# A latent convolution in 32x32 tiles of the TensorE array, and a layer norm with channels on the partitions

## The chip, the cores and the metric

The kernel runs on one core of one Trainium2 chip. The core has five engines that run their own instruction queues and meet at semaphores: TensorE (PE in the profile; PEld is its weight load), VectorE (DVE), ScalarE (ACT), GpSimd (POOL) and SyncE (SP), which here issues every DMA. Each engine takes its instructions in the order in which they stand in its queue. The metric is the time of one execution on the device in microseconds. Before the change it is 1876.82 us, the median of three runs (1874.78 to 1887.96).

## What is computed

One layer of a hybrid backbone over 2304 tokens (256 of a prompt, 2048 of a 32x64 grid of latents): an input projection, an SSD (Mamba-2) branch in both directions, a conformer branch, and an output projection over both branches. The change concerns the conformer branch alone:

```
def depthwise_conv(x, w, b):            # 31 taps along the rows of the grid
    k, ch = w.shape
    out = lax.conv_general_dilated(
        x, w.reshape(k, 1, 1, ch).astype(x.dtype), window_strides=(1, 1),
        padding=((k // 2, k // 2), (0, 0)),
        dimension_numbers=('NHWC', 'HWIO', 'NHWC'), feature_group_count=ch)
    return out + b.astype(x.dtype)
...
def conformer_branch(ga, gb, conv_w, conv_b, ln_g, ln_b):
    h = ga * jax.nn.sigmoid(gb)
    h = depthwise_conv(h, conv_w, conv_b)
    h = layer_norm(h, ln_g, ln_b)
    return jax.nn.silu(h)
...
    y_conf = y_conf.reshape(bsz, seqlen, D_CONF) * jax.nn.silu(gsil)
    out = jnp.concatenate([y_ssd.astype(x.dtype), y_conf.astype(x.dtype)], axis=-1) @ w_out
    return x + gate * rms_norm(out, g_post), h_fin
```

For the latents the grid has 32 rows and 64 columns, so the convolution of one channel is a 32x32 banded matrix applied to 64 columns. There are 1024 channels. The layer norm runs over the 1024 channels of a token.

## The kernel before

Tokens are handled in 18 tiles of 128 (two of the prompt, sixteen of the latents), channels in 8 groups of 128. The input projection runs in two halves of the tokens. In each half, units of matmuls of 128x512 (`xbc_unit`, `gab_unit`, `silu_unit`, with the matmuls on L378 to L380, three for each piece since every weight and activation is split in a high and a low part) form the backbone of TensorE's work, and smaller work is put between them: the forward scan (`pass_a`), the prompt's convolution on VectorE (`ctx_conv`) and the latent convolution on TensorE (`lat_conv`). `gab_unit` writes the gated channels to the DRAM buffers `GL[j]`.

`lat_conv(j)` runs for each group of 128 channels, in the second half of the tokens. It loads the banded matrices (`kd`) and the input (`x`) so that four channels share the 128 partitions, four times 32 rows of the grid. ScalarE spreads each block of 32x32 into a block diagonal matrix in one of two zeroed buffers `kbuf` (`expand`, L622, 16 copies for a group). A matmul on L634 then has `x` as its weights (128 rows, 64 columns) and `kbuf` as its moving operand (128 columns), and gives the result with the 64 grid columns on the partitions. VectorE adds the bias (L639), and two DMAs write the result to `CVL`, token by token.

The second stage, from about 1420 us to the end, is the output projection, one tile of 128 tokens after the other. For each tile there are 96 matmuls of 128x512 on L1078 (`out_part`): 48 on the SSD half `yh`, `yl`, 48 on the conformer half `ph`, `pl`. Between them the next tiles are prepared: `ssd_pre`, `ssd_norm`, `ssd_scale` for the SSD half; `conf_pre` loads a tile of the convolution's result with tokens on the partitions and normalizes it by statistics along the free axis (L1042 to L1047; the power of -0.5 of 128 single numbers is on POOL, L135), and `conf_act` turns it to channels on the partitions by eight transposes on TensorE (L1058), applies scale, bias and SiLU on ScalarE (L1061) and multiplies by the gate (L1063). `conf_hl` splits the result in `ph` and `pl`. The tiles `cn` (normalized), `v`, `ph`, `pl` have one buffer each.

The source sets what is computed and which buffers are used, and a list scheduler, which plays the program through with its own cost estimates when the program is built, sets the order of the instructions in each engine's queue. So the order of a queue is not the order of the source, and it is shown below, from the built programs.

Of the kernel before, what the change touches and what calls it, by code (L numbers as in the profile page):

```python
# [67 lines left out]
def backbone_kernel(ctx, tc, xa, xt_in, cols, rows, wconv, conf_b, gp_row, bg_row, state0, w_mod, w_dt, w_in, w_out,  # L68
# [458 lines left out]

    def gab_unit(half, j, hb):
        wb = next_w()
        wa = next_w()  # L530
        for b in ORDER[half]:
# [48 lines left out]
    def ctx_conv(j, tile):  # L580
# [22 lines left out]
    def lat_conv(j, lp, kbuf):  # L603
        cbb = lp.tile([P, HD], F32, tag="cbb", name=f"cbb{j}", bufs=2)
        for h in range(2):
            c0 = j * P + h * 64
# [8 lines left out]
        for c4 in range(4):
            DMA.dma_start(x[c4 * 32:(c4 + 1) * 32], src[c4])

        def expand(u):
            kt = kbuf[u % 2]
            for c4 in range(4):  # L620
                rs = slice(c4 * 32, (c4 + 1) * 32)
                S.copy(kt[rs, :, rs].rearrange("p (h q) r -> p h q r", h=2),  # L622
                       kd[rs].rearrange("p r (h u q) -> p u h q r", h=2, u=4)[:, u])
# [606 lines left out]
```

## Time and profile before

| what | value |
|---|---|
| median of three runs | 1876.82 us |
| the profiled execution, its own time | 1882.2 us |
| its span in the profile | 1880.5 us |
| TensorE busy | 1825.6 us, 97% of the span |
| VectorE, ScalarE, GpSimd busy | 63%, 45%, 14% |
| granted TensorE clock, mean | 0.986 |

In the profile a line such as L1078 is a line of the kernel before. Busy time of TensorE is time in which some matmul is under way; matmuls overlap, so the start of one to the start of the next, not the duration, says what one costs. A matmul of two float32 operands is two instructions in the trace (hence x16 for eight), one of float32r operands is one.

### The profile page before, as it was taken

How to read it: one execution, taken by the hardware profiler on the slowest of the kernel's cores; microseconds unless marked ns; L12 is line 12 of the kernel's file. 1: busy time of each engine (PE TensorE's matmuls, PEld its weight loads, DVE VectorE, ACT ScalarE, POOL GpSimd, SP SyncE). 2: the span in 40 equal slices, each digit the busy share in tenths (PEclk: the TensorE clock that was granted, in tenths of full speed). 3: DMA queues.
4: the chain of work that ended last, by engine and by line, in shares of the span. 5: the costliest groups of instructions: out<-in, count | busy, mean ns of one | idle time of the engine just before them, and what ended most of it. 6: DMA issues, size and time to landing. Idle time of an engine off the chain costs nothing.

```text
span 1880.5 us, 26833 instructions
## 1 busy us (share of the span) xinstructions
PE 1825.6 (97%) x9739; PEld 1504.6 (80%) x9739; DVE 1188.2 (63%) x1699; ACT 839.5 (45%) x1786; POOL 269.0 (14%) x351
## 2 busy tenths in 40 slices
PE   7899999999999999999999899999999999999998
PEld 4788887787887888888877677777887888888887
DVE  2477887776545553577585768655427676766662
ACT  3646424443455441644355666675414232232321
POOL 0002001111111100100001011110013333333220
PEclk9899999999999999999999999999999999999999
DMA  8556575564677754545587897978887655555532
GB/s 302 212 200 198 211 239 179 176 222 155 211 269 225 225 200 169 165 154 188 179 195 215 210 242 194 278 185 234 239 268 239 191 174 173 165 172 173 175 102 78
DMA packets 290400, 375.29 MB, mean 200 GB/s; under 512 B 85206, under 2 KB 187478, under 8 KB 290268
## 3 DMA queue, kind: packets, MB, share of 16 engines
q1 hardware_dynamic: 290268, 373.58, 64.2%
q8 instruction: 77, 1.26, 0.3%
q14 instruction: 55, 0.45, 0.1%
HBM read 243.92 MB, written 129.59 MB: 199 GB/s over the span
## 4 chain that ended last, share of the span: by engine, by line
PE 62%; DMA 5%; ACT 3%; issue 3%; DVE 2%; SPq 2%; POOL 0%; POOLq 0%; DVEq 0%; ACTq 0%
PE op L1078 20%; PE sp L378 6%; PE sp L379 6%; PE sp L380 6%; DMA lb<-lt 3%; PE xp L379 2%; PE xp L378 2%; PE xp L380 2%; PE py L720 2%; PE ga L378 2%; PE ga L380 1%; PE po L727 1%; PE ga L379 1%; PE qo L985 1%; PE gb L378 1%
## 5 line engine op out<-in xcount | busy, mean ns | idle before, releaser
L684 ACT ACTIVATE lb<-lb,WB 128x128 f32<-128x128 f32 x576 | 184.1, 391 | 150.9 <-POOL lb L676 149.0
L378 PE MATMUL sp<-hh,wh 128*128 128x512 f32 (+1 forms) x640 | 239.7, 375 | 2.6 <-DVE sth L550 2.6
L379 PE MATMUL sp<-hl,wh 128*128 128x512 f32 (+1 forms) x640 | 237.0, 370 | 0.0
L380 PE MATMUL sp<-hh,wl 128*128 128x512 f32 (+1 forms) x640 | 236.7, 370 | 0.2 <-DMA wl<-wld 0.2
L676 POOL TENSOR_SCALAR_AFFINE_SELECT lb<-lb 128x512 f32<-128x512 f32 x144 | 108.7, 760 | 749.7 <-ACT el L673 416.1
L378 PE MATMUL xp<-hh,wh 128*128 128x512 f32 (+1 forms) x480 | 179.1, 375 | 6.1 <-ACT wh L353 4.0
L379 PE MATMUL xp<-hl,wh 128*128 128x512 f32 (+1 forms) x480 | 179.1, 373 | 0.2 <-DVE hl L299 0.2
L380 PE MATMUL xp<-hh,wl 128*128 128x512 f32 (+1 forms) x480 | 179.2, 374 | 0.0
L475 DVE SCALAR_TENSOR_TENSOR cva<-raw,cwh,cva 128x1280 f32<-128x1280 f32 (+1 forms) x96 | 142.7, 1495 | 15.5 <-ACT cva L469 13.6
L378 PEld LDWEIGHTS sp<-hh,wh 128*128 128x128 f32 x640 | 121.0, 189 | 24.3 <-DVE sth L550 3.1
L380 PEld LDWEIGHTS sp<-hh,wl 128*128 128x128 f32 x640 | 121.0, 189 | 21.6 <-DMA wl<-wld 0.7
L379 PEld LDWEIGHTS sp<-hl,wh 128*128 128x128 f32 x640 | 121.2, 189 | 20.1 <-issue 0.5
L378 PE MATMUL gb<-hh,wh 128*128 128x512 f32 (+1 forms) x320 | 121.9, 381 | 3.4 <-DVE gth L539 3.4
L378 PE MATMUL ga<-hh,wh 128*128 128x512 f32 (+1 forms) x320 | 120.4, 376 | 2.6 <-ACT gth L536 2.6
L379 PE MATMUL gb<-hl,wh 128*128 128x512 f32 (+1 forms) x320 | 119.3, 373 | 0.0
L380 PE MATMUL gb<-hh,wl 128*128 128x512 f32 (+1 forms) x320 | 119.1, 372 | 0.0
L380 PE MATMUL ga<-hh,wl 128*128 128x512 f32 (+1 forms) x320 | 118.1, 369 | 0.0
L379 PE MATMUL ga<-hl,wh 128*128 128x512 f32 (+1 forms) x320 | 117.9, 369 | 0.0
L590 DVE SCALAR_TENSOR_TENSOR cg<-cg,cv 128x256 f32<-128x256 f32 x240 | 113.3, 497 | 2.5
L550 DVE SCALAR_TENSOR_TENSOR sth<-sth,sp 128x512 f32<-128x512 f32 (+1 forms) x80 | 50.4, 630 | 98.4 <-ACT sth L549 98.4
L378 PEld LDWEIGHTS xp<-hh,wh 128*128 128x128 f32 x480 | 92.0, 192 | 23.0 <-ACT wh L353 4.8
L688 DVE TENSOR_TENSOR lb<-lb,lb 128x512 f32<-128x512 f32 x72 | 51.6, 717 | 85.6 <-ACT lb L684 55.8
(219 smaller groups left out, 3860.8 us busy)
## 6 DMA issues: line engine op xcount, KB each, us to landing
lb<-lt SPq DMA_DIRECT2D x144, 256.0 KB, 4.2
wr<-in_w_in SPq DMA_DIRECT2D x88, 256.0 KB, 4.9
whd<-wh SPq DMA_DIRECT2D x44, 512.0 KB, 3.4
wld<-wl SPq DMA_DIRECT2D x44, 512.0 KB, 4.7
wh<-whd SPq DMA_DIRECT2D x44, 512.0 KB, 5.2
wl<-wld SPq DMA_DIRECT2D x44, 512.0 KB, 5.6
xT<-xb SPq DMA_DIRECT2D x18, 512.0 KB, 5.4
yp<-yg SPq DMA_DIRECT2D x36, 256.0 KB, 4.5
```

The source lines that it names most:

```text
L378: T.matmul(ps[:, :BN], wh[:, k, :], hh[:, k, :], start=(k == 0), stop=False)
L379: T.matmul(ps[:, :BN], wh[:, k, :], hl[:, k, :], start=False, stop=False)
L380: T.matmul(ps[:, :BN], wl[:, k, :], hh[:, k, :], start=False, stop=(k == KT - 1))
L475: V.scalar_tensor_tensor(a[:, :n], raw[:, t:t + n], cwh[:, ct * 5 + t:ct * 5 + t + 1], a[:, :n], MUL, ADD)
L550: V.scalar_tensor_tensor(th, th, 1.0, ps[:, :BN], ADD, MUL)
L590: V.scalar_tensor_tensor(acc, g[:, t:t + 256], cv[:, w0 + t:w0 + t + 1], acc, MUL, ADD)
L676: G.affine_select(E[g, hq, d], E[g, hq, d], pattern=[[0, 4], [sg, P]], compare_op=ALU.is_ge, fill=NEG, base=0, channel_multiplier=-sg)
L684: S.activation(lb[:, h, :], lb[:, h, :], AF.Exp, bias=WB[:, i, c + h:c + h + 1])
L688: V.tensor_tensor(a, a, E[g, hq, 1], ADD)
L720: T.matmul(py[g][j * HD:(j + 1) * HD, q * P:(q + 1) * P], xt[g][:, h * HD:(h + 1) * HD], E[g, hq, 0][:, t, :], start=True, stop=True)
L727: T.matmul(po[g][:, q * P:(q + 1) * P], Sf[g][:, q * P:(q + 1) * P], bc[:, 2 + g, :], start=True, stop=True)
L1078: T.matmul(pso[n], lhs[:, k % 8, :], w[:, n * 512:(n + 1) * 512], start=(k == 0 and m == 0), stop=(k == 15 and m == 2))
```

## The change

The convolution's weights are no longer block diagonal. Each matmul now takes one channel: a 32x32 banded matrix `kt` as weights in one 32x32 tile of the array, and the channel's 32 rows by 64 columns as the moving operand. Four channels stand on four groups of rows (`a`), and four groups of columns (`u`) give 16 places, of which a run of 64 matmuls uses two row groups and four column groups. There are 128 such matmuls for a group of 128 channels where there were 32. One copy on ScalarE reverses the band; `expand` and `kbuf` are gone; loads are issued a group ahead where `GL[j]` is complete (`lat_load`, `gl_done`), in 16 pieces instead of 4, and results are written in 8 pieces instead of 2. Results stand in one buffer `CV` with channels as rows, and the prompt's convolution writes there too, without its two transposes for a group.

In the output stage a tile is loaded with channels on the partitions (`conf_load`). The sum over 1024 channels is taken by three additions on VectorE and a matmul with ones (`quarter_sum`), once for the mean and once for the squares, which gives the sum on all partitions. The power of -0.5 on POOL is taken of 128x128 numbers. The eight transposes go. The steps are `conf_load`, `conf_mean`, `conf_var`, `conf_act`.

```diff
-    kbuf = [lp.tile([P, 8, P], F32, name=f"kbuf{u}") for u in range(2)]
-    for u in range(2):
-        G.memset(kbuf[u], 0.0)
...
@@ ctx_conv
-        ps = bank("ss", f"cps{j}")
-        for t in range(2):
-            T.transpose(ps[:, t * P:(t + 1) * P], acc[:, t * P:(t + 1) * P], ident)
         o = g[:, 768:1024]
-        S.mul(o, ps[:, :256], 0.5)
+        S.mul(o, acc, 0.5)
+        DMA.dma_start(CV[j * P:(j + 1) * P, 0:256], o)
...
@@ lat_conv (the old body is printed above)
+    def lat_load(j, lp):
+        kd = lp.tile([P, 32, 32], F32, tag="kd", name=f"kd{j}", bufs=2)
+        x = lp.tile([P, 32, 64], F32, tag="cx", name=f"cx{j}", bufs=2)
+        lat_in[j] = kd, x
+        for a in range(4):
+            rs = slice(a * 32, (a + 1) * 32)
+            src = bass.AP(tensor=wconv.tensor, offset=(j * 4 + a) * 64 * 32, ap=[[32, 32], [1, 1024]])
+            DMA.dma_start(kd[rs].rearrange("p r g -> p (r g)"), src)
+            for u in range(4):
+                c0 = u * 32 + a * 8
+                DMA.dma_start(x[rs, u * 8:(u + 1) * 8, :],
+                              GL[j][c0:c0 + 8, 256:].rearrange("c (r w) -> r c w", w=64))
+
+    def lat_conv(j, lp, cbb, more):
+        if j not in lat_in:
+            lat_load(j, lp)
+        kd, x = lat_in.pop(j)
+        yield
+        kt = lp.tile([P, 32, 32], F32, tag="kt", name=f"kt{j}", bufs=1)
+        S.copy(kt[:, :, ::-1].rearrange("p g r -> p r g"), kd)
+        if more(j + 1):
+            lat_load(j + 1, lp)
+        yield
+        vt = lp.tile([P, 32, 64], F32, tag="cvv", name=f"cvv{j}", bufs=1)
         for h in range(2):
+            ps = {a: bank("ss", f"cp{j}_{a}") for a in (2 * h, 2 * h + 1)}
+            for q in range(8):
+                for u in range(4):
+                    for a in ps:
+                        rs = slice(a * 32, (a + 1) * 32)
+                        T.matmul(ps[a][u * 32:(u + 1) * 32, q * 64:(q + 1) * 64], kt[rs, u * 8 + q, :], x[rs, u * 8 + q, :],
+                                 start=True, stop=True)
             yield
+            for a in ps:
+                V.scalar_tensor_tensor(vt[:, a * 8:(a + 1) * 8, :], ps[a].rearrange("p (c w) -> p c w", w=64), 0.5,
+                                       cbb[:, j, a * 8:(a + 1) * 8].unsqueeze(2).to_broadcast([P, 8, 64]), MUL, ADD)
+            for u in range(4):
+                c0 = j * P + u * 32 + h * 16
+                DMA.dma_start(CV[c0:c0 + 16, 256:].rearrange("c (r w) -> r c w", w=64),
+                              vt[u * 32:(u + 1) * 32, h * 16:(h + 1) * 16, :])
+            yield
...
+    def quarter_sum(t, v, name):
+        V.tensor_tensor(t, v[:, 0:4, :], v[:, 4:8, :], ADD)
+        V.tensor_tensor(t[:, 0:2, :], t[:, 0:2, :], t[:, 2:4, :], ADD)
+        V.tensor_tensor(t[:, 0, :], t[:, 0, :], t[:, 1, :], ADD)
+        ps = bank("ss", name)
+        T.matmul(ps[:, 0:P], ones, t[:, 0, :], start=True, stop=True)
+        return ps[:, 0:P]
...
+    def conf_mean(i, n):
+        v = p2.tile([P, 8, P], F32, tag="v", name=f"v{i}", bufs=1)
+        mean = quarter_sum(v[:, 0:4, :], n, f"cm{i}")
+        V.scalar_tensor_tensor(n, rows8(mean), -1.0 / D, n, MUL, ADD)
+        return n, v
+
+    def conf_var(i, nv):
+        n, v = nv
+        S.activation(v, n, AF.Square)
+        var = quarter_sum(v[:, 0:4, :], v, f"cq{i}")
+        r = p2.tile([P, P], F32, tag="cr", name=f"cr{i}", bufs=1)
+        V.tensor_scalar(r, var, 1.0 / D, EPS, MUL, ADD)
+        G.tensor_tensor(r, r, nhalf.to_broadcast([P, P]), ALU.pow)
+        V.tensor_tensor(n, n, rows8(r), MUL)
+        return n, v
...
@@ the loop over tiles
-            n = conf_pre(nxt)
-        out_part(pso[i], yh, 3, 6)
+            n = conf_load(nxt)
+        out_part(pso[i], yh, 3, 5)
         if not last:
             yhn = ssd_scale(nxt, yr)
-        out_part(pso[i], yh, 6, 8)
+        out_part(pso[i], yh, 5, 7)
+        if not last:
+            n = conf_mean(nxt, n)
+        out_part(pso[i], yh, 7, 8)
         out_part(pso[i], pt, 8, 10)
...
+            n = conf_var(nxt, n)
+            out_part(pso[i], pt, 10, 12)
             v = conf_act(nxt, n)
-            out_part(pso[i], pt, 10, 16)
+            out_part(pso[i], pt, 12, 16)
```

Three places of the built programs show how the queues change. The first is VectorE in the output stage, one tile of the steady part, before the change (lines of the kernel before; `bs`, `mv` and `cn` are the layer norm of one tile, `elb`, `y`, `z`, `zr` the SSD half of a tile two ahead, `o` the output being finished, `v` the conformer half):

```order
L1063 SCALAR_TENSOR_TENSOR v_13650<-v_13650,gsl_13648 128x1024
L1042 BN_STATS bs_13784<-cn_13782 128x6 x2
L1044 BN_AGGR mv_13787<-bs_13784 128x2
L1045 TENSOR_SCALAR mv_13787<-mv_13787 128x1
L1047 TENSOR_SCALAR cn_13782<-cn_13782,mv_13787,cr_13790 128x1024
L1070 TENSOR_TENSOR pl_13721<-v_13650,ph_13720 128x1024
L1006 TENSOR_SCALAR yms_13734<-pm_13732 128x1
L1088 TENSOR_TENSOR oms_13709<-oms_13709 128x1
L1089 TENSOR_SCALAR oms_13709<-oms_13709 128x1
```

The same queue with the change (lines of the changed kernel: L1068 gives the variance `cr` from the sum `cq`, L1070 multiplies the tile by its power, which POOL has taken in between, L1111 begins the finish of the output):

```order
L1068 TENSOR_SCALAR cr_15724<-cq_15722 128x128
L1010 TENSOR_SCALAR yms_15803<-pm_15801 128x1
L1105 TENSOR_TENSOR oms_15778<-oms_15778 128x1
L1106 TENSOR_SCALAR oms_15778<-oms_15778 128x1
L990 TENSOR_TENSOR elb_15821<-elb_15821,qo_15830 128x512
L990 TENSOR_TENSOR elb_15821<-elb_15821,qo_15836 128x512
L991 TENSOR_TENSOR y_15824<-y_15824,elb_15821 128x1024
L992 TENSOR_TENSOR y_15824<-y_15824,z_15826 128x1024
L995 TENSOR_REDUCE zr_15845<-z_15826 128x128
L1070 TENSOR_TENSOR cn_15661<-cn_15661,cr_15724 128x1024
L1111 SCALAR_TENSOR_TENSOR o_15777<-op_0_15603,or_15783,gg_13855 128x512
L1111 SCALAR_TENSOR_TENSOR o_15777<-op_1_15604,or_15783,gg_13855 128x512
```

Before, the layer norm of a tile stood in one piece and ended with `cn`, a tile ahead of its use; now its second half is spread over the tile's row, with the SSD half's work between `cr` and the multiplication.

The second place is TensorE in the same part, one tile with the change (`cm` and `cq` are the two sums over channels, `ph_15789` is the conformer half that comes out of the layer norm whose sums these are, `op` the output's banks):

```order
L1095 MATMUL op_1_15604<-woh_13814,ph_15599 128x512
L1047 MATMUL cm_15697<-v_15693,ones 128x128
L1095 MATMUL op_0_15603<-wol_13813,ph_15599 128x512
...
L1095 MATMUL op_1_15604<-wol_13849,ph_15599 128x512
L1047 MATMUL cq_15722<-v_15693,ones 128x128
L1095 MATMUL op_0_15603<-woh_13850,pl_15600 128x512
...
L1016 MATMUL pm_15801<-ident,yr_15805 128x128
...
L1095 MATMUL op_0_15793<-woh_13509,ph_15789 128x512
```

Between `cm` and `cq` stand 38 matmuls on L1095 (the former L1078), between `cq` and the first one on `ph_15789` 35 with the matmuls of `qo` and `pm`, and between that one and the next tile's `cm` 24. Before the change the same stretch held one interruption, and it came half a tile or more before its result was used:

```order
L1078 MATMUL op_0_13917<-woh_13066,pl_13914 128x512
L1078 MATMUL op_1_13918<-woh_13066,pl_13914 128x512
L1058 MATMUL ct_14037<-ident,cn_13975 128x128 x4
L1058 MATMUL ct_14046<-ident,cn_13975 128x128 x4
L1078 MATMUL op_0_13917<-woh_13072,ph_13913 128x512
L1078 MATMUL op_1_13918<-woh_13072,ph_13913 128x512
```

The eight transposes `ct` are gone, and two single matmuls have come, each of which waits for VectorE and is waited for by it.

The third place is the queue of DMAs (SP) during the latent convolution, with the change (`lb` are rows of decays that the forward scan loads and waits for, `cx` and `kd` the convolution's inputs, `cv` its results):

```order
L599 DMA cv<-cg_11250 128x256
L666 DMA lb_10049<-lt_116 128x512
L617 DMA cx_9768<-gl_71 32x8x64 x16
L645 DMA cv<-cvv_9834 32x16x64 x4
L666 DMA lb_10114<-lt_116 128x512
L666 DMA lb_10437<-lt_116 128x512
L599 DMA cv<-cg_12388 128x256
```

Here 20 DMAs of the convolution stand between two loads of the scan. In the queue before, the same loads and stores of a group (two halves) read like this:

```order
L616 DMA cx_9617<-gl_70 32x32x64 x2
L644 DMA cvl<-cvv_9297 64x32x64 x2
L616 DMA cx_9617<-gl_70 32x32x64 x2
L664 DMA lb_9716<-lt_117 128x512
L607 DMA cbb_10325<-in_conf_b 64x64 x2
L664 DMA lb_9799<-lt_117 128x512
```

The loads of the scan have moved behind longer groups of smaller DMAs.

More of the change, by code (lines that the diff above doesn't have):

```diff
@@ L526, in xbc_phase @@
             pass
+    gl_done = set()
     def gab_unit(half, j, hb):
@@ L530, in gab_unit @@
         wa = next_w()
+        gl_done.discard(j)
         for b in ORDER[half]:
@@ L540, in gab_unit @@
             DMA.dma_start(GL[j][:, o:o + BN], th)
+        if half:
+            gl_done.add(j)
     def silu_unit(half, c0, dst, j, hb, order=None):
@@ L928, in backbone_kernel @@
     lp = ph_l.enter_context(tc.tile_pool(name="lp", bufs=1, side="right"))
-    kbuf = [lp.tile([P, 8, P], F32, name=f"kbuf{u}") for u in range(2)]
-    for u in range(2):
-        G.memset(kbuf[u], 0.0)
+    cbb = lp.tile([P, 8, 32], F32, name="cbb")
+    for u in range(4):
+        DMA.dma_start(cbb[u * 32:(u + 1) * 32],
+                      conf_b.rearrange("(j u n) -> u j n", u=4, n=32)[u].partition_broadcast(32))
     blocks = post(1, 5)
     cg = lambda name: lp.tile([P, D], F32, tag="cg", name=name, bufs=2)
-    extra = chain(f for j in range(4) for f in (lat_conv(2 * j, lp, kbuf), ctx_conv(j + 4, cg), lat_conv(2 * j + 1, lp, kbuf)))
+    lat = lambda j: lat_conv(j, lp, cbb, gl_done.__contains__)
+    extra = chain(f for j in range(4) for f in (lat(2 * j), ctx_conv(j + 4, cg), lat(2 * j + 1)))
     sc_ = scan(range(9, NT))
@@ L1035, in load_gg @@
         gg[a] = t
-    def conf_pre(i):
-        n = p2.tile([P, D], F32, tag="cn", name=f"cn{i}", bufs=1)
-        DMA.dma_start(n, CVC[i * P:(i + 1) * P, :] if i < 2 else CVL[(i - 2) * P:(i - 1) * P, :])
-        bs = p2.tile([P, 12], F32, tag="bs", name=f"bs{i}", bufs=2)
-        for h in range(2):
-            V.bn_stats(bs[:, 6 * h:6 * h + 6], n[:, h * 512:(h + 1) * 512])
-        mv = p2.tile([P, 2], F32, tag="mv", name=f"mv{i}", bufs=2)
-        V.bn_aggr(mv, bs)
-        V.tensor_scalar(mv[:, 1:2], mv[:, 1:2], EPS, None, ADD)
-        r = rstd_of(p2, mv[:, 1:2], f"cr{i}")
-        V.tensor_scalar(n, n, mv[:, 0:1], r, SUB, MUL)
-        return n
@@ L1051, in conf_act @@
+    def conf_act(i, nv):
+        n, v = nv
         gs = p2.tile([P, 8, P], F32, tag="gs", name=f"gsl{i}", bufs=1)
         DMA.dma_start(gs, chan_slice(GS, i))
-        v = p2.tile([P, 8, P], F32, tag="v", name=f"v{i}", bufs=1)
-        for g in range(2):
-            ps = bank("ss", f"ct{i}{g}")
-            for c in range(4):
-                k = 4 * g + c
-                T.transpose(ps[:, c * P:(c + 1) * P], n[:, k * P:(k + 1) * P], ident)
-            for c in range(4):
-                k = 4 * g + c
-                S.activation(v[:, k, :], ps[:, c * P:(c + 1) * P], AF.Silu, bias=cv[:, C_LNB + k:C_LNB + k + 1],
-                             scale=cv[:, C_LNG + k:C_LNG + k + 1])
+        for k in range(8):
+            S.activation(v[:, k, :], n[:, k, :], AF.Silu, bias=cv[:, C_LNB + k:C_LNB + k + 1],
+                         scale=cv[:, C_LNG + k:C_LNG + k + 1])
```

56 lines of the change are left out of this document (9 added, 47 removed).

## The prediction

> **What bounds the kernel now.** I read the page first: the shares of the engines and the chain that ended last.
>
> ```profile
> span 1880.5 us, 26833 instructions
> ...
> PE 1825.6 (97%) x9739; PEld 1504.6 (80%) x9739; DVE 1188.2 (63%) x1699; ACT 839.5 (45%) x1786; POOL 269.0 (14%) x351
> ...
> PE 62%; DMA 5%; ACT 3%; issue 3%; DVE 2%; SPq 2%; POOL 0%; POOLq 0%; DVEq 0%; ACTq 0%
> ```
>
> TensorE (PE) is busy for 97% of the span and carries most of the chain. That is an average, so I then took four windows: the half in which the latent convolution runs, a short stall with what follows it, and twelve tiles of the output stage. Columns are start and end, length, busy time of each engine (instructions), clock, DMA.
>
> ```profile
> core 0: us, PE busy (x) PEld busy (x) DVE busy (x) ACT busy (x) POOL busy (x), PEclk, DMA share, GB/s
> 925.00:1345.00 420.00, 402.55 (x2378) 316.66 (x2377) 275.43 (x451) 253.72 (x566) 44.56 (x70) 0.98 0.81 218
> 1443.00:1446.90 3.90, 1.29 (x5) 0.41 (x3) 3.86 (x4) 3.81 (x8) 1.49 (x1) 1.00 0.63 182
> 1446.90:1453.80 6.90, 5.91 (x14) 4.65 (x15) 6.90 (x7) 3.22 (x6) 0.00 (x0) 0.51 0.58 185
> 1479.10:1779.10 300.00, 300.00 (x1490) 253.03 (x1490) 207.63 (x242) 87.97 (x182) 102.07 (x84) 1.00 0.57 174
> ```
>
> In the output stage PE never rests: 300.00 of 300.00 us, at full clock. It is twelve tiles long (the reduction L991 below runs 12 times in it), so a tile takes 25.0 us. VectorE works 207.63/12 = 17.3 us of that, ScalarE 7.3, POOL 8.5. A change that only takes work from PE would gain here; a change that makes PE wait for VectorE loses what it waits.
>
> **The output stage, step by step.** The timeline of PE gives prices by starts (x2 is two matmuls of float32r, or one of float32):
>
> ```profile
> 1608.68 1.95 PE L985 MATMUL qo<-ct,Sb 128*128 128x128 f32 x16
> 1610.38 0.71 PE L1078 MATMUL op<-woh,yh 128*128 128x512 f32 x2
> 1610.93 0.62 PE L1078 MATMUL op<-wol,yh 128*128 128x512 f32 x2
> ...
> 1613.65 0.61 PE L1078 MATMUL op<-wol,yh 128*128 128x512 f32 x2
> ...
> 1614.56 0.38 PE L1012 MATMUL pm<-ident,yr 128*128 128x128 f32 x2
> 1614.70 0.70 PE L1078 MATMUL op<-woh,yh 128*128 128x512 f32 x2
> ...
> 1620.27 1.03 PE L1058 MATMUL ct<-ident,cn 128*128 128x128 f32 x8
> 1621.06 0.70 PE L1078 MATMUL op<-woh,ph 128*128 128x512 f32 x2
> 1621.60 0.63 PE L1078 MATMUL op<-wol,ph 128*128 128x512 f32 x2
> ```
>
> From 1610.93 to 1613.65 stand six pairs: 2.72/12 = 0.227 us for an output matmul. A pair behind float32 work starts its successor 0.54 us later, not 0.455, so a switch costs 0.08. The eight transposes of a tile (x8, one instruction each) cost 0.79 + 0.08 = 0.87. One matmul with ones has the shape of `pm`: 0.14 + 0.08 = 0.22. So the change takes 0.87 and adds 0.44: PE alone would gain 0.4 us a tile.
>
> VectorE and ScalarE, from their groups in the same 300 us (busy, mean ns of one, idle before it and its releaser):
>
> ```profile
> L988 DVE TENSOR_TENSOR y<-y,z 128x1024 f32<-128x1024 f32 x13 | 27.6, 2120 | 3.4 <-DMA y<-yp 3.0
> L991 DVE TENSOR_REDUCE zr<-z 128x128 f32<-128x1024 f32 x12 | 24.2, 2020 | 0.0
> L987 DVE TENSOR_TENSOR y<-y,elb 128x1024 f32<-128x1024 f32 x12 | 21.1, 1756 | 0.4
> L1094 DVE SCALAR_TENSOR_TENSOR o<-op,or,gg 128x512 f32<-128x512 f32 x24 | 16.9, 747 | 11.1 <-POOL or L135 11.1
> L986 DVE TENSOR_TENSOR elb<-elb,qo 128x512 f32<-128x512 f32 x24 | 15.3, 681 | 0.0
> ...
> L1063 DVE SCALAR_TENSOR_TENSOR v<-v,gsl 128x1024 f32<-128x1024 f32 x12 | 14.7, 1225 | 44.1 <-ACT v L1061 44.1
> ...
> L1013 DVE TENSOR_TENSOR y<-y,pm 128x1024 f32<-128x1024 f32 x12 | 14.5, 1208 | 0.0
> ...
> L1006 DVE TENSOR_SCALAR yms<-pm 128x1 f32<-128x1 f32 x12 | 1.8, 152 | 0.0
> ...
> L1061 ACT ACTIVATE v<-ct,cv 128x128 f32<-128x128 f32 x96 | 34.9, 471 | 37.6 <-PE ct L1058 37.6
> ...
> L989 ACT ACTIVATE z<-y 128x1024 f32<-128x1024 f32 x13 | 13.8, 1062 | 114.7 <-DVE y L988 114.7
> L1069 ACT CAST ph<-v 128x1024 fp32r<-128x1024 f32 x13 | 13.7, 1054 | 63.6 <-PE op L1078 48.4 <-DVE cn L1047 10.4 <-DVE bs L1042 4.8
> ```
>
> In the changed order a tile's layer norm is a closed loop: PE does `cm`; VectorE takes the mean; ScalarE squares; PE does `cq` 38 output matmuls later; VectorE, POOL, VectorE, ScalarE, VectorE and ScalarE follow one another up to the next `ph`; and 24 output matmuls after its first use stands the next `cm`. With one buffer each for `cn`, `v` and `ph` nothing overlaps a turn with the next one.
>
> *`cm` to `cq`:* 0.22 + 38 x 0.227 = 8.9 us on PE. Beside it VectorE has the subtraction of the mean (1.23 by L1063), ScalarE the square (1.06), VectorE three additions (at most 0.68 each by L986): under 5.4 us, hidden behind the 38.
>
> *`cq` to the first matmul on `ph`:* 0.39 for `cq` and the way to VectorE (the x2 at 1614.56 lasts 0.38), the variance 0.27 (128x128, between 0.152 and 0.681, nearer the small one), three small instructions 0.45, then `qo`, which ends about 2.9 us after the start of `cq` (0.22, a few output matmuls, and 1.70 for its sixteen), so 0.9 of waiting; then 2 x 0.68, 1.76, 2.12, the square of `z` 1.06 with 0.1 on the way, the reduction 2.02: 10.4 us by now. The product with the power 1.2 (by L1013), then 2 x 0.747, 1.21 (L1013) and 1.225 of the finish, in whose shade ScalarE does eight SiLUs (8 x 0.36 = 2.9 back to back, 3.8 at 471 ns): 3.9. Then 1.23 for the gate and 1.05 for `ph`. Sum 17.8 us. PE has for this stretch 35 output matmuls, `qo` and `pm`: 8.0 + 1.7 + 0.3 = 10, and idles 7.8.
>
> *`ph` to the next `cm`:* 24 x 0.227 = 5.5 us.
>
> The turn is 8.9 + 17.8 + 5.5 = 32.2 us instead of 25.0: +7.2. For 17 turns +122; the first tile's chain has no tile before it to hide behind, 0 to 18 us, I take the middle, +9. Late next, once PE waits, is nothing else: the loads of `yp` and of the tile have more time than before.
>
> **Clock.** The windows above show PE at 0.51 for 6.9 us after a stretch in which it was busy for 1.29 of 3.90 us. An idle time of 7.8 us a tile is longer. Of the next 6.9 us half would be lost if PE set the time, 3.4 a tile; but the 24 matmuls (5.5 us) are what lies on the loop there, and part of those 38. Bounds 0 and 3.4 a tile; I take a third, 1.2, since the slow stretch can also fall in the idle time itself: +20. The Trainium skill ("TensorE: Matmul & The Clock Gate", Part 1) has half clock after an idle window of about 3.4 us and full clock after a busy one as long; the 0.51 agrees, the 6.9 us is two such windows, and by the page the estimate is 1.7 us a tile, +29 where I have +20.
>
> **POOL.** The power goes from one number a partition to 128.
>
> ```profile
> L123 POOL MEMSET nhalf<- 128x1 f32 x1 | 0.1, 98 | 0.0
> ...
> L135 POOL TENSOR_TENSOR cr<-mv,nhalf x18: 547/548/1459, 1409.0 to 1825.0; 128x1 f32<-128x1 f32 x18
> ...
> L997 POOL TENSOR_TENSOR Sb<-Sb,eTb x34: 1037/1044/2065, 1363.9 to 1809.3; 128x512 f32<-128x512 f32 x34
> ```
>
> A power of one number takes 548 ns, a memset of one 98, and a product of 512 numbers 1044, about 2 ns each. So the power's price p lies between 0.548 + 127 x 0.002 = 0.8 us, if the 450 ns above the memset are a start, and 0.1 + 128 x 0.45 = 57.7 us, if each number pays them. It is issued when the variance is there and needed for the product 9.8 us later (the 10.4 less what stands ahead of it): that work of the SSD half covers it up to p = 9.8, and costs it at nothing. Behind it on POOL wait the powers of the other norms and the products on `Sb`; they are wanted in the same stretch in which PE idles. No row says where between 0.8 and 57.7 p lies. I take it as covered, by the nearest shape (L997, four times as many numbers in 1.04 us), and this is the weakest step: the other end is a rival of nearly the same chance.
>
> **The latent convolution.**
>
> ```profile
> 957.53 0.39 PE L380 MATMUL ga<-hh,wl 128*128 128x512 f32 x1
> 957.85 1.09 PE L634 MATMUL cp<-kbuf,cx 128*64 128x128 f32 x16
> 958.87 0.50 PE L378 MATMUL ga<-hh,wh 128*128 128x512 f32 x1
> 959.21 0.40 PE L379 MATMUL ga<-hl,wh 128*128 128x512 f32 x1
> ...
> 28.03 0.61 PE L239 MATMUL mp<-wm,sc 128*2 128x256 f32 x8
> ...
> PE cp L634 <- ACT kbuf L622: 10.0, 6, 2.7
> ...
> L616 SPq DMA_DIRECT2D cx<-gl x32: 325/637/2844, 946.1 to 1290.8; - x32
> ```
>
> A run of eight now is 1.02 us with 0.20 for the switches: 32 runs, 39 us. Of small tiles of the array only L239 has something: eight instructions on 256 columns in four places, 0.61 with 0.38 for the last, so 0.23 for four, 58 ns each, 14 ns for 64 columns. The 16 new runs have 128 instructions each (64 matmuls): 16 x (128 x 0.0144 + 0.2) = 33 us, -6. The bound above is L634's own 64 ns each: 16 x (8.2 + 0.2) = 134, +95. I take the small one since it is the row with several tiles. The Trainium skill ("TensorEngine Tiling (Array Packing)", Instruction Overhead) gives a matmul about 60 cycles however short; an estimate by it is 25 ns each, 55 us for the runs, and +22 in the sum; no run of short instructions in this trace shows which holds. The waits for `kbuf` go, -10, and the 16 transposes of the prompt's part, 16 x 0.1 by L1058 and eight switches, -2. Issues on SP: 14 more of them stand ahead of a scan's load in each of 8 groups, 14 x 0.325 = 4.6 us each, 36 if all shows and 0 if the load was early enough; I take the middle, +18.
>
> **Sum:** 122 + 9 + 20 - 6 - 10 - 2 + 18 = +151. The profiled execution took 1882.2 us, 1.7 over its span and 5 over the median of 1876.8: 2033, or 2028 on the scale of the median, which I round to 2030.
>
> **Rivals.** *The power is the bound.* From p = 9.8 us on, `cq` to `ph` is 8.0 + p (0.66 for `cq` and variance, then p, 1.2, 3.9, 1.23, 1.05), and each us above costs 17. For it speaks that 450 of the 548 ns are the power's own; against, that a start can be long. p = 57.7 gives 2030 + 48 x 17 = 2840; between 9.8 and 57.7 by ratio lies 24, 2270.
> *The other side, not slower.* If the chain from `cq` to `ph` fits in the 10 us that PE has there, PE stays the bound: 24.6 us a tile, -7, with -18 for the latent part and without the +18, 1850. It decides when the chain is 8 us shorter than summed. Against it stand the five large instructions of VectorE between the variance and the product, 9 us by themselves.
> *Short matmuls cost 64 ns.* +101 on the forecast, 2130.
> *The change's matmuls don't run side by side, but the loop is looser than summed* (VectorE takes the product earlier): 1900 to 1990.
>
> **Chances and range.** Forecast 0.44, with its own range 1990 to 2100; the power 0.41; the other side 0.05; 64 ns 0.05; looser 0.05. Low 1985 leaves out the other side and most of the looser loop, 0.08; high 2600 (p = 43) leaves out the last part of the power's ratio, ln(57.7/43)/ln(57.7/9.8) x 0.41 = 0.07. About 1% is what a measurement of this kernel can tell from no change: faster 0.03 and same 0.03 come from the other side and the loosest of the loops, slower 0.94 from the rest.
>
> **What would show it.** In twelve tiles of the changed kernel: a period near 32 us; PE idle about 8 us a tile ahead of the first `ph`, put down to the cast or VectorE; clock near 0.5 behind it; the power under 9.8 us, with VectorE not waiting for POOL at the product. The power right up to the product, POOL busy most of a tile, and VectorE's idle time put down to `cr` would be the rival. The runs on the latent line should be near 2 us long. What would make it wrong: the power's price first, then that `cm` or `cq` waits too.

## The result, and the profile after

The changed kernel takes 2289.22 us, the median of four runs (2288.09 to 2291.74), against 1878.82 us for the kernel before on the same chip: a ratio of 1.2175 with a 95% interval of 1.2148 to 1.2203. It is slower by a fifth. 2030 us was forecast, so the direction was right and the size was not: the loss is 410 us where about 150 were summed. The time lies in the range that was given, which reached to 2600 for one rival's sake, and it is that rival that came true.

The page of the changed kernel, with its span, the shares of the engines, the chain that ended last, and three of the costliest groups:

```profile
span 2290.0 us, 29847 instructions
...
PE 1877.9 (82%) x11187; PEld 1531.7 (67%) x11187; DVE 1238.7 (54%) x1771; ACT 797.7 (35%) x1684; POOL 625.6 (27%) x349
...
PE 63%; issue 14%; DMA 7%; DVE 6%; POOL 5%; ACT 3%; SPq 1%; POOLq 0%; DVEq 0%; ACTq 0%
...
L1069 POOL TENSOR_TENSOR cr<-cr,nhalf 128x128 f32<-128x128 f32 x18 | 374.4, 20799 | 349.4 <-DVE cr L1068 347.6
...
L1016 PE MATMUL pm<-ident,yr 128*128 128x128 f32 x36 | 13.9, 489 | 227.8 <-POOL yr L134 227.8
...
L1070 DVE TENSOR_TENSOR cn<-cn,cr 128x1024 f32<-128x1024 f32 x18 | 22.9, 1272 | 220.7 <-POOL cr L1069 220.7
```

TensorE (PE) went from 97% of the span to 82%; its busy time rose by only 52 us. POOL's busy time more than doubled, from 269 to 626 us, and one line of it is new: the power on L1069, 18 times 20.8 us. Both VectorE (at the product, L1070) and PE (at L1016) waited for POOL for some 220 us. PE's wait is for another power, `yr` of the SSD half, which stands behind the long one in POOL's queue.

One tile of the steady part, from one second sum `cq` to the next tile's `cm` and a little beyond, in the timeline of all engines (start, duration, engine, line, operation; in brackets the idle time before it and what ended it):

```profile
1720.12 0.38 PE L1047 MATMUL cq<-v,ones 128*128 128x128 f32 x2
...
1720.91 20.75 POOL L1069 TENSOR_TENSOR cr<-cr,nhalf 128x128 f32<-128x128 f32 x1 [19.91 <-DVE cr L1068]
...
1724.19 0.69 DVE L990 TENSOR_TENSOR elb<-elb,qo 128x512 f32<-128x512 f32 x1 [1.73 <-PE qo L989]
...
1727.07 1.22 DVE L992 TENSOR_TENSOR y<-y,z 128x1024 f32<-128x1024 f32 x1
...
1729.42 1.87 DVE L995 TENSOR_REDUCE zr<-z 128x128 f32<-128x1024 f32 x1 [1.13 <-ACT z L993]
...
1741.63 0.54 POOL L134 TENSOR_TENSOR yr<-yms,nhalf 128x1 f32<-128x1 f32 x1
1741.68 1.23 DVE L1070 TENSOR_TENSOR cn<-cn,cr 128x1024 f32<-128x1024 f32 x1 [10.39 <-POOL cr L1069]
...
1742.22 0.80 PE L1016 MATMUL pm<-ident,yr 128*128 128x128 f32 x2 [12.62 <-POOL yr L134]
...
1743.28 2.04 POOL L1001 TENSOR_TENSOR Sb<-Sb,eTb 128x512 f32<-128x512 f32 x2
1743.35 1.41 DVE L1111 SCALAR_TENSOR_TENSOR o<-op,or,gg 128x512 f32<-128x512 f32 x2 [0.44 <-POOL or L134]
...
1745.29 3.48 POOL L1002 TENSOR_TENSOR Sb<-Sb,stl 128x512 f32<-128x512 f32 x2
1745.80 1.83 DVE L1115 TENSOR_TENSOR o<-o,xr 128x1024 f32<-128x1024 f32 x1
...
1747.18 1.22 PE L1095 MATMUL op<-woh,yh 128*128 128x512 f32 x2 [4.17 <-ACT yh L1023]
1747.56 2.29 DVE L1080 SCALAR_TENSOR_TENSOR v<-v,gsl 128x1024 f32<-128x1024 f32 x1
...
1750.98 1.22 PE L1095 MATMUL op<-woh,ph 128*128 128x512 f32 x2 [1.73 <-ACT ph L1086]
...
1752.00 1.05 PE L1095 MATMUL op<-wol,ph 128*128 128x512 f32 x2
...
1752.86 1.05 PE L1095 MATMUL op<-woh,yl 128*128 128x512 f32 x2
...
1759.04 0.38 PE L1047 MATMUL cm<-v,ones 128*128 128x128 f32 x2
```

VectorE is done with the SSD work at 1731.29 and then sits idle for 10.39 us until the power ends. The product follows at once, and from there to the first matmul on `ph` the chain is as forecast in its order: 9.3 us. PE is idle for 12.6 us, then 4.2, then 1.7. The same tile by stretches shows what this does to the clock:

```profile
core 0: us, PE busy (x) PEld busy (x) DVE busy (x) ACT busy (x) POOL busy (x), PEclk, DMA share, GB/s
1711.24:1720.12 8.88, 8.88 (x42) 7.36 (x41) 2.64 (x4) 1.06 (x1) 0.00 (x0) 1.00 0.00 0
1720.12:1729.00 8.88, 8.88 (x51) 7.69 (x50) 4.59 (x8) 1.94 (x5) 8.09 (x1) 1.00 0.11 30
1729.00:1748.00 19.00, 2.21 (x7) 1.40 (x6) 7.75 (x7) 4.51 (x10) 19.00 (x7) 0.58 0.24 55
1748.00:1759.00 11.00, 9.27 (x28) 6.86 (x28) 5.60 (x6) 1.04 (x1) 0.77 (x1) 0.65 0.84 277
```

From the first variance at 1432.7 us to the last at 2240.6 (L1068) are 17 turns of 47.5 us, where a tile took 25.0 before. That is 17 x 22.5 = 383 of the 410 us. The rest is mostly in the projection phase: from the last matmul on `xp` to the last on `sp` it took 502.4 us before (917.1 to 1419.5) and takes 518.3 now (912.2 to 1430.5), 16 us more. The 11 us that are left, in the first tile and at the ends of the output stage, were not taken apart.

### The profile page after: what moved, and what is told of

It is laid out like the page before. It is cut to its first block, busy times and chain, and to the rows that moved or that the text cites. A ratio compares the mean times of both kernels' runs of the same rounds, so it can differ in the third digit from the quotient of the medians.

```text
span 2290.0 us, 29847 instructions
## 1 busy us (share of the span) xinstructions
PE 1877.9 (82%) x11187; PEld 1531.7 (67%) x11187; DVE 1238.7 (54%) x1771; ACT 797.7 (35%) x1684; POOL 625.6 (27%) x349
## 4 chain that ended last, share of the span: by engine, by line
PE 63%; issue 14%; DMA 7%; DVE 6%; POOL 5%; ACT 3%; SPq 1%; POOLq 0%; DVEq 0%; ACTq 0%
PE op L1095 13%; PE sp L377 5%; PE sp L378 5%; PE sp L379 5%; PE xp L377 4%; PE xp L378 4%; PE xp L379 4%; POOL cr L1069 4%; DMA lb<-lt 3%; PE gb L377 2%; PE gb L378 2%; PE gb L379 2%; PE ga L377 2%; PE ga L378 2%; PE ga L379 2%
## 5 line engine op out<-in xcount | busy, mean ns | idle before, releaser
L1069 POOL TENSOR_TENSOR cr<-cr,nhalf 128x128 f32<-128x128 f32 x18 | 374.4, 20799 | 349.4 <-DVE cr L1068 347.6
L1016 PE MATMUL pm<-ident,yr 128*128 128x128 f32 x36 | 13.9, 489 | 227.8 <-POOL yr L134 227.8
L1095 PE MATMUL op<-woh,yh 128*128 128x512 f32 x288 | 114.7, 448 | 66.6 <-ACT yh L1023 66.6
L1016 PEld LDWEIGHTS pm<-ident,yr 128*128 128x128 f32 x36 | 8.9, 305 | 234.7 <-POOL yr L134 234.7
L1078 ACT ACTIVATE v<-cn,cv 128x128 f32<-128x128 f32 x144 | 57.4, 480 | 265.1 <-DVE cn L1070 265.1
L1070 DVE TENSOR_TENSOR cn<-cn,cr 128x1024 f32<-128x1024 f32 x18 | 22.9, 1272 | 220.7 <-POOL cr L1069 220.7
L1095 PE MATMUL op<-woh,ph 128*128 128x512 f32 x288 | 100.7, 430 | 50.2 <-ACT ph L1086 50.1
```

What stands on the lines that cost most here:

```text
L1016: T.matmul(pm[:, P:2 * P], r.to_broadcast([P, P]), ident, start=True, stop=True)
L1069: G.tensor_tensor(r, r, nhalf.to_broadcast([P, P]), ALU.pow)
L1070: V.tensor_tensor(n, n, rows8(r), MUL)
L1078: S.activation(v[:, k, :], n[:, k, :], AF.Silu, bias=cv[:, C_LNB + k:C_LNB + k + 1], scale=cv[:, C_LNG + k:C_LNG + k + 1])
L1095: T.matmul(pso[n], lhs[:, k % 8, :], w[:, n * 512:(n + 1) * 512], start=(k == 0 and m == 0), stop=(k == 15 and m == 2))
```

## The experiments

Ten kernels were run, each with the kernel before beside it on the same chip. Ratios are to it, with their intervals.

| kernel | median us | ratio to before | a tile, us |
|---|---|---|---|
| the change | 2289.2 | 1.2175 (1.2148 to 1.2203) | 47.5 |
| pow_half | 2112.2 | 1.1231 (1.1208 to 1.1255) | 37.9 |
| pow_one | 1973.4 | 1.0492 (1.0467 to 1.0516) | 30.4 |
| tok_early | 2008.0 | 1.0671 (1.0643 to 1.0698) | 32.4 |
| early22 | 1900.2 | 1.0107 (1.0088 to 1.0127) | 25.0 |
| ahead | 1895.2 | 1.0072 (1.0056 to 1.0088) | 25.1 |
| ahead_pow | 2051.4 | 1.0913 (1.0893 to 1.0933) | 33.7 |
| ahead_lat | 1880.8 | 1.0003 (0.9992 to 1.0014) | 25.1 |
| lat4 | 2280.5 | 1.2123 (1.2098 to 1.2148) | as the change |
| warm44 | 2314.4 | 1.2307 (1.2284 to 1.2330) | 47.8 |
| warm61 | 2306.0 | 1.2263 (1.2229 to 1.2297) | 46 to 48 |

A tile is 1/17 of the time from the first variance to the last; for early22, ahead and ahead_lat the distance of two casts to `ph` in the steady part, and for the two warm kernels that of two `cm` there (47.8 in the change, by the same measure).

### Is it the power? A smaller one in the same order

```diff
-        G.tensor_tensor(r, r, nhalf.to_broadcast([P, P]), ALU.pow)
+        G.tensor_tensor(r[:, 0:64], r[:, 0:64], nhalf.to_broadcast([P, 64]), ALU.pow)
```

> The power is taken of 64 of the 128 columns; the other 64 tokens of a tile are scaled by the variance itself, so that half of the layer norm is left out. VectorE's order is the one of the changed kernel. Theory A (the power of 128x128, 20.8 us, is on the loop for all that passes the 11.2 us of VectorE's work beside it): the power lasts 10.4 us, the product stands about where VectorE's other work ends, a tile falls from 47.6 to about 37 us, the whole by 10.4 x 18 = 187 us, to about 2100 us. Theory B (the power has a large start and the loop of single buffers is what costs): the power stays near 20 us or the tile stays above 44 us, 2230 us or more. If PE's idle time gets short enough for full clock, another 2 us a tile goes, and it is about 2065.

The power's rows, of pow_half and of pow_one below (min/median/max in ns, first and last start):

```profile
L1069 POOL TENSOR_TENSOR cr<-cr,nhalf x18: 10529/10542/10542, 1427.2 to 2071.4; 128x64 f32<-128x64 f32 x18
```

```profile
L1069 POOL TENSOR_TENSOR cr<-cr,nhalf x18: 549/550/1399, 1425.1 to 1941.1; 128x1 f32<-128x1 f32 x18
```

Theory A holds. Half the columns take half the time, so the power has no large start: (20.746 - 10.542)/64 = 0.159 us for each column, and (10.542 - 0.55)/63 = 0.159 again. The time fell by 177 us to 2112, which is 17 turns by the 10.2 us that the power got shorter, 173, within 4. VectorE's order up to the product is that of the change, and its wait there is down to 0.2 us in one steady tile and 2.2 in the next: the power now ends about where VectorE's other work ends. All waits at the product together are 49.2 us, the most that covering the rest of the power could give back, so 2112 is within that of what this loop takes with the power fully covered.

### With no power to speak of

```diff
-        G.tensor_tensor(r, r, nhalf.to_broadcast([P, P]), ALU.pow)
+        G.tensor_tensor(r[:, 0:1], r[:, 0:1], nhalf, ALU.pow)
```

> The power is taken of one column of 128; 127 of 128 tokens of a tile are scaled by the variance itself. The order changes with it: the product now stands before most of the SSD work on VectorE. Theory A: the power is 0.55 us, the chain from the second sum to the first matmul on ph is some 9 us, about what PE has to do there, so PE is the bound again at about 25 us a tile: 1878.8 - 7 for the transposes + 16 for the latent phase = about 1890 us (1875 to 1920). Theory B (the closed loop of single buffers costs even without the power, the 32 us a tile of the prediction): 2030 us.

Neither theory was right. With the short power the list scheduler puts the product 0.95 or 1.88 us behind the variance (start to start) instead of behind the SSD work, so the loop gets shorter than the forecast's; but a tile still takes 30.4 us, not 25. What PE waits for in the output stage has moved (engine, line waited for, us in total, times, longest):

```profile
PE op L1095 <- ACT yh L1023: 48.2, 15, 5.7
PE op L1095 <- ACT ph L1086: 8.3, 10, 2.2
PE op L1095 <- DVE yl L1024: 5.2, 6, 1.1
```

Now the SSD half `yh` is late, because VectorE does the layer norm first and had stood idle for `cm` and `cq` before (3.5 and 4.8 us in one tile). A tile still takes about 5 us more than before the change, which the power doesn't explain.

### What is left without the power: one buffer or two

The next two kernels compute the whole layer. The variance of each token is summed with one column of ones, so that it stands on 128 partitions, the power is of 128x1, and a matmul spreads it:

```diff
-        var = quarter_sum(v[:, 0:4, :], v, f"cq{i}")
-        r = p2.tile([P, P], F32, tag="cr", name=f"cr{i}", bufs=1)
-        V.tensor_scalar(r, var, 1.0 / D, EPS, MUL, ADD)
-        G.tensor_tensor(r, r, nhalf.to_broadcast([P, P]), ALU.pow)
-        V.tensor_tensor(n, n, rows8(r), MUL)
+        pv = quarter_col(v[:, 0:4, :], v, f"cq{i}")
+        r = p2.tile([P, 1], F32, tag="cr", name=f"cr{i}", bufs=1)
+        V.tensor_scalar(r, pv[:, 0:1], 1.0 / D, EPS, MUL, ADD)
+        G.tensor_tensor(r, r, nhalf, ALU.pow)
+        T.matmul(pv[:, P:2 * P], r.to_broadcast([P, P]), ident, start=True, stop=True)
+        V.tensor_tensor(n, n, rows8(pv[:, P:2 * P]), MUL)
```

In tok_early the steps of the next tile's layer norm also stand earlier in the source: `conf_load` ahead of the first output matmul, `conf_mean` after the second group of `yh`, `conf_var` after the fifth.

> Complete computation. The second sum is taken with one column of ones, so the variances of 128 tokens stand on 128 partitions; POOL's power is of 128x1, and a matmul spreads it over the channels. The mean and the variance of the next tile stand earlier in the tile. Theory A: the power is 0.55 us, PE never waits for long, 25 us a tile, about 1890 us; with the mean and the variance early not above 1895. Theory B: single buffers hold the chain back, above 1950 us.

2008 us, in the range of theory B, and slower than pow_one, which leaves the steps where the change has them. One reading is that writing the steps earlier can't make them run earlier while `cn` and `v` of the tile in hand are still in use. So early22 is the same source with two buffers:

```diff
-        n = p2.tile([P, 8, P], F32, tag="cn", name=f"cn{i}", bufs=1)
+        n = p2.tile([P, 8, P], F32, tag="cn", name=f"cn{i}", bufs=2)
...
-        v = p2.tile([P, 8, P], F32, tag="v", name=f"v{i}", bufs=1)
+        v = p2.tile([P, 8, P], F32, tag="v", name=f"v{i}", bufs=2)
```

> As tok_early, with two buffers each for cn and v in place of one; nothing else is changed in the source. Theory F (what is left of the loss without the power is the closed loop of single buffers: the next tile's mean can't start before this tile's v is read out): a tile falls from 33 to 25 us, PE waits for almost nothing, 17 x 8 = 136 us less than tok_early's 2008, about 1875 us (1860 to 1900). Theory G (VectorE's work is too much or too badly placed, beside POOL's products on Sb that slow it): the buffers help little, 1960 us or more.

1900.2 us, 108 less than tok_early, at the upper edge of what theory F gave. The window of twelve tiles of early22 shows PE without a pause and at full clock, as before the change:

```profile
core 0: us, PE busy (x) PEld busy (x) DVE busy (x) ACT busy (x) POOL busy (x), PEclk, DMA share, GB/s
1480.00:1780.00 300.00, 300.00 (x1465) 250.91 (x1464) 231.51 (x289) 104.34 (x192) 108.73 (x85) 1.00 0.58 173
```

VectorE is busy 231.5 of these 300 us, more than the 207.6 before, and it doesn't matter: theory G falls. What cost was the closed loop. With the second buffers the scheduler also gave VectorE's queue another order (the next tile's mean now stands ahead of the end of this tile's SSD work); the 108 us are those of the buffers with the order that they allow. A kernel with the mean taken a whole tile ahead of its variance, and one with the same and the long power, complete the picture:

```diff
...
-            n = conf_load(nxt)
+            nl = conf_load(order[a + 2])
...
-            n = conf_mean(nxt, n)
+            n = conf_var(nxt, nrm)
...
+                nrm = conf_mean(order[a + 2], nl)
```

> Complete computation, power of 128x1, two buffers for cn and v, and the mean of a tile taken a whole tile earlier than its variance. Theory F: PE is the bound at 24.6 to 25 us a tile, as early22 or up to 10 us better: 1865 to 1890 us. Theory G: 1960 us or more.

> As ahead, but with the power of 128x128 of the changed kernel. Theory A with F: POOL has 20.8 us of power and 7 us of other work for a tile, and the chain from the variance to ph is at least 27 us, so a tile takes 28 to 34 us: 1930 to 2040 us, far under the 2289 of the changed kernel, since two buffers let the power of one tile stand beside the matmuls of another. If the single buffers alone were the cause, about 1880 us; if the power can't be covered at all, near 2289.

ahead took 1895.2 us, 5 us over the upper end of what was expected and 5 better than early22. ahead_pow took 2051.4, 11 over its range: a tile is 33.7 us in the mean, 23.4 and some 46 in alternation. With two buffers, and the mean taken a tile earlier, the power of 20.7 us lies beside the matmuls of another tile, which gives back 238 of the change's 410 us. In what stays, POOL's queue has a large part: POOL is busy for 397 of the 500 us from 1480 on, the short power for `yr` and the products on `Sb` still stand behind the long one, and PE waits 39.1 us in all for `yr` and 40.4 for `ph`. So the power alone, or the single buffers alone, would have cost about 156 us (ahead_pow against ahead) or 108 us (tok_early against early22); together they cost some 390 us (the change against ahead). These are estimates, since ahead also has the mean a tile earlier, and no run has the long power and single buffers in that order.

### The projection phase

The loads of the latent convolution go in four DMAs a group instead of sixteen:

```diff
-            for u in range(4):
-                c0 = u * 32 + a * 8
-                DMA.dma_start(x[rs, u * 8:(u + 1) * 8, :],
-                              GL[j][c0:c0 + 8, 256:].rearrange("c (r w) -> r c w", w=64))
+            DMA.dma_start(x[rs], GL[j][rs, 256:].rearrange("c (r w) -> r c w", w=64))
```

> The latent convolution's input is loaded in 4 DMAs a group instead of 16, with the same bytes; the rows of channels are then in another order than the weights, so the latent convolution's values are of wrong pairs. Theory C (the 16 us that the projection phase lost are SP's: the scan's loads stand behind more issues): ScalarE's wait for the loads of the scan falls from 99 to below 60 us, the phase up to the output stage gets 10 to 20 us shorter, about 2275 us. Theory D (the loss comes from where the list scheduler put VectorE's work around the new matmuls, or from the clock): within 5 us of 2289.

2280.5 us, 8.7 less than the change: between the two theories. ScalarE's wait for the scan's loads fell from 99.5 to 75.9 us, not below 60. The second kernel makes the same loads valid by giving the gate products' channels another order on the host side (in the columns of the input weights and in the prompt's convolution), and writes the result in 4 DMAs instead of 8 (the prompt's part in 4 instead of 1):

```diff
+    pos = np.arange(P).reshape(4, 4, 8).transpose(1, 0, 2).reshape(-1)
...
-            for u in range(4):
-                c0 = j * P + u * 32 + h * 16
-                DMA.dma_start(CV[c0:c0 + 16, 256:].rearrange("c (r w) -> r c w", w=64),
-                              vt[u * 32:(u + 1) * 32, h * 16:(h + 1) * 16, :])
+        for u in range(4):
+            c0 = j * P + u * 32
+            DMA.dma_start(CV[c0:c0 + 32, 256:].rearrange("c (r w) -> r c w", w=64), vt[u * 32:(u + 1) * 32])
```

> Complete computation: as ahead, with the channels of the gate products in such an order that the latent convolution's input comes in 4 DMAs a group instead of 16, and its result goes in 4 instead of 8; the prompt's part is written in 4 instead of 1. Theory C (SP's issues): 8 to 16 us less than ahead, 1855 to 1875 us, below the kernel before. Theory D (order of VectorE's work): the same as ahead within 4 us.

1880.8 us, 14.5 less than ahead, as theory C had it, but 5.8 above the range of times given for it, since ahead itself came out later. The waits of ScalarE between 912 and 1300 us name the place: it waits for the scan's loads `lb` when it makes the decays `el` from them. First the kernel before, then the change, then ahead_lat:

```profile
ACT el L673 <- DMA lb<-lt: 28.2, 12, 6.1
```

```profile
ACT el L675 <- DMA lb<-lt: 99.5, 19, 11.9
```

```profile
ACT el L673 <- DMA lb<-lt: 63.4, 16, 10.9
```

An `lb` load itself takes as long as ever (4.3 us from issue to landing on the page, 4.2 before); it is issued later. With fewer issues in front of it the wait falls by 37 us (in ahead it was 100.2, as in the change) and the time by 14.5; ScalarE's wait for POOL's part of the same rows rose meanwhile, from 57.8 to 83.0 us. Theory C holds in kind: the number of DMAs costs. How much of the 16 us it is stays less certain. In the profiled executions the projection phase takes 506.4 us in lat4 (518.3 in the change) and 506.5 in ahead_lat (511.7 in ahead), so 5 to 12 us, and 4 more than before are left. And the kernels with all the loads and no idle matmuls, whose latent convolution is the same, differ among themselves from 511.7 to 518.3 us, so what the scheduler places around it has a share too, as theory D had it. ahead_lat, which does all that the change meant to do, is as fast as the kernel before and not faster: 1.0003 with an interval of 0.9992 to 1.0014. No version was found that is faster than the kernel before.

### The clock behind an idle time

44 matmuls without use wait for the reduction L995 and fill PE's long idle stretch, without moving any instruction of the other engines in the steady part:

```diff
+        if not first:
+            wm = bank("ss", f"wm{i}")
+            for _ in range(44):
+                T.matmul(wm[:, 0:P], zr, ident, start=True, stop=True)
```

> The changed kernel, with 44 idle matmuls of 128x128 (float32, result unused) that wait for the reduction of the tile's squares and so stand in PE's idle time ahead of the matmul on the power yr; the order of all other engines is unchanged. Theory H (the half clock behind the long idle time costs what the 24 matmuls from ph to the next sum take over 5.5 us, 2.6 us a tile): PE is busy through most of the 12.8 us, the clock stays at full, a tile falls from 47.6 to about 45 us, 17 x 2.6 = 44 us, about 2245 us. Theory I (the idle time of 4.2 us before yh alone brings the half clock, or the matmuls wait for something else): within 10 us of 2289. If the idle matmuls delay yh, up to 2310.

Theory I: a tile stays at 47.8 us. The median is 25 us above the change's; between the two profiled executions the difference is 18 us, and 19 come in the first tile, where the idle matmuls stand in the way (from its `cq` to the next `cm` 60 us instead of 40.7). In the timeline of PE in warm44 the fillers run at full clock (88 instructions in 10.09 us, granted clock 1.00), and after 4.47 us without work the next matmuls are slow all the same:

```profile
1749.61 10.09 PE L999 MATMUL wm<-ident,zr 128*128 128x128 f32 x88 [1.75 <-DVE zr L995]
1760.49 0.49 PE L1020 MATMUL pm<-ident,yr 128*128 128x128 f32 x2 [0.78 <-POOL yr L134]
1765.45 1.22 PE L1099 MATMUL op<-woh,yh 128*128 128x512 f32 x2 [4.47 <-ACT yh L1027]
1766.47 1.05 PE L1099 MATMUL op<-wol,yh 128*128 128x512 f32 x2
```

So warm61 fills that stretch as well, with 17 more behind the matmul on `yr`:

```diff
         T.matmul(pm[:, P:2 * P], r.to_broadcast([P, P]), ident, start=True, stop=True)
+        wn = bank("ss", f"wn{i}")
+        for _ in range(17):
+            T.matmul(wn[:, 0:P], r.to_broadcast([P, P]), ident, start=True, stop=True)
```

> As warm44, with 17 more idle matmuls behind the one on the power yr, so that PE is busy in the second idle stretch of a tile too (4.5 us in warm44, up to the matmul on yh). Theory H2 (an idle stretch of 4.5 us is enough for half clock, and the half clock costs what the matmuls from yh to the next sum take over their full-clock time): the clock stays at full, ph to the next sum falls from 8.1 to 5.5 us, a tile from 47.8 to about 45.2, the whole by 17 x 2.6 = 44 us against warm44's 2314, about 2270 us. Theory I2 (the slow matmuls there have another cause than idle time, such as what they read): a tile stays at 47.8 us, 2305 to 2320.

```profile
1766.67 5.28 PE L1023 MATMUL wn<-ident,yr 128*128 128x128 f32 x34
1771.71 0.71 PE L1102 MATMUL op<-woh,yh 128*128 128x512 f32 x2
...
1773.69 0.73 PE L1102 MATMUL op<-woh,ph 128*128 128x512 f32 x2 [0.80 <-ACT ph L1093]
...
1776.56 0.62 PE L1102 MATMUL op<-woh,yh 128*128 128x512 f32 x2
```

The clock is back: the matmul pairs stand 0.455 us apart instead of 0.85. In the tile shown, the 25 output matmuls from `ph` to `cm` take 5.8 us (granted clock 1.00), where the change takes 8.06, so half clock costs 2.3 us a tile, some 39 us in all. The total fell by only 8 us against warm44, a miss. In most of the other tiles the scheduler put 29 to 32 matmuls into that stretch instead of 25 (7.4 us at full clock for 32), which ate most of the gain: the turns from the second variance on got 12 us shorter in all, and what stands ahead of them 8 us longer. The size of the clock's share is thus read from one tile and from the spacing; a whole run that shows only it was not had.

## Why the prediction was wrong

The step that failed is the one named as the weakest there: "I take it as covered, by the nearest shape (L997, four times as many numbers in 1.04 us)". The power's price p had been bounded between 0.8 and 57.7 us and was set at the small end by a row of another operation. It is 20.75 us. The row of the operation itself, 548 ns for one number beside 98 for a memset, was the better guide: the power takes 0.55 us for one column and 0.159 us for each further one, 20.75 us for 128. The 450 ns above the memset were partly a start and partly the price of a number.

Point by point, with the tile that the timeline shows:

- *`cm` to `cq`, 8.9 us:* 8.88. Right.
- *The cover of 9.8 us:* VectorE was done with the SSD work 10.4 us after the power began in the tile shown, and 8.4 in the one beside it (the wait at the product is 10.4 us in one tile and 12.4 in the next, of 20.75). Right on the mean, 9.4, and so was the point from which the power decides; pow_half, at 10.5 us, stands on it. But there was luck in it. The two operations on `y` (L991, L992) took 1.2 us each, not the 1.76 and 2.12 summed, while in the tile shown VectorE could begin on `qo` only 4.1 us after `cq`, not 2.0 (2.1 in the tile beside it). The two errors offset each other.
- *The product, forecast 10.4 us after `cq`:* 21.56. Of the 14.1 us by which a turn exceeds 32.2 + 1.2, this is 11.2, all of it the power.
- *From the product to `ph`, 7.4 us:* 9.3. Mis-sized by 1.9. VectorE waited 0.44 us for the power `or` of the output's norm, and the finish and the gate took 1.83 and 2.29 us instead of 1.225, while POOL's products on `Sb`, held back behind the long power, now stand beside them. "Behind it on POOL wait the powers of the other norms and the products on `Sb`; they are wanted in the same stretch in which PE idles" was half right: the power for `yr` held PE at L1016 too, in the shade of the other wait.
- *`ph` to `cm`, 5.5 us and 1.2 for the clock:* 8.06. The mechanism was right; the term was mis-sized by 1.4 us a tile: not "a third" but some two thirds of the 3.4 (2.3 by warm61).
- *The latent part, summed to 0 (-18 and +18):* +16. The runs came out at 1.40 us, shorter than the 1.84 summed, and PE's waits for `kbuf` are gone, as said. The rival of 64 ns a matmul falls, since 128 instructions in 1.40 us are 11 ns each. The estimate of 25 ns by the Trainium skill ("TensorEngine Tiling (Array Packing)", Instruction Overhead) falls by the same number. Worked back, what ate the savings is 16 + 18 = 34 us, where 18 had been summed, all of it for SP. That all 34 are SP's is not shown: 8.7 came back in lat4 and 14.5 in ahead_lat. Beside SP, PE's waits in this phase for the convolution's own bias addition `cvv` went from 0.3 to 12 us, and the granted clock there went from 0.98 to 0.95; PE was busy as long as before (484 us) and idle for 34.5 us instead of 17.7.
- *PE's saving:* 0.4 us a tile was expected from the transposes once PE is the bound. In ahead, where it is, a tile takes 25.13 us against 24.99. The three small float32 matmuls there take 0.67 us by their starts where the eight transposes took 0.87, so 0.2 us is saved; but the output matmuls on `ph` and `pl` stand 0.233 us apart instead of 0.228, and those on `yh` and `yl` 0.230 instead of 0.228, some 0.35 us for the 96 of a tile. Why they stand wider is open.

The sum of these: 17 x 14.1 = 240, and 16 for the projection phase, 256 of the 259 us between 2030 and 2289. The rival of the power gave 2030 + 17 x (20.75 - 9.8) = 2216 at the price that was measured; the 73 us from there to 2289 are the other points.

What the forecast had right is shown by the other runs: the single buffers close a loop (tok_early against early22, 108 us). Whether the latent convolution would gain by itself, with the old layer norm, was not tried: its result has the channels on the partitions, and the old stage wants tokens there.

The Trainium skill ("TensorE: Matmul & The Clock Gate", Part 1) has half clock after an idle window of about 3.4 us; 4.47 us of idle time in warm44, behind 10 us of dense work, agree with it: the granted clock is 0.50 over the next 8.3 us.

## What to carry to other kernels

An operation that is cheap on one number for each partition is no small operation: before it is widened, find its price for each element, and if only one point is known, let the row of that operation and not a similar shape set the forecast. Keep statistics in the layout in which there are few of them, and spread the result with a matmul (0.55 us and one small matmul instead of 20.75 us). And a chain that ends in the tile that the next turn reads needs a second buffer before it needs a better order in the source: with the steps written earlier a tile still took 32.4 us, and with two buffers 25.0.

## What the runs showed of the hardware that was not expected

POOL's power is linear: 0.55, 10.54 and 20.75 us for 1, 64 and 128 columns. Beside it VectorE is not slowed, and beside POOL's products on `Sb` it is. Before the change `y*z` (L988) mostly begins while one of these products is running and takes 2.19 us, and the gate (L1063) never does and takes 1.22. In the change the products on `Sb` have moved behind the power: `y*z` (L992) takes 1.22 us beside the power, and the gate (L1080) takes 2.29 in the steady tiles, where a product on `Sb` is running as it begins. In the tile shown that product ends 1.2 us after the gate's start, and the gate 1.1 us after that, as if it had begun only then. The other way round there is no loss for VectorE: before the change the finish begins 0.8 us ahead of a product on `Sb` and takes 1.22 us. And 32x32 tiles of the array do run side by side. In this row of the changed kernel 128 instructions stand between two of 128x512, 11 ns each for 64 columns, where L634 before the change, without such tiles, took 64 ns for 128 columns:

```profile
952.88 1.47 PE L637 MATMUL cp<-cx,kt 32*32 32x64 f32 x128
954.28 0.50 PE L377 MATMUL ga<-hh,wh 128*128 128x512 f32 x1
```
